# A scheduler flag, and the block inverses of a delta rule: substitution in blocks of 16, the doubling from 16 to 32 on TensorE, and other amounts of filler work between the steps

## The chip, the cores and the metric

The kernel runs on one core of one Trainium2 chip. The metric is device microseconds (us) of one execution. TensorE does the matrix products and the transposes against an identity; VectorE and ScalarE evacuate PSUM, cut weights into two parts and do the elementwise steps; GpSimd (POOL) has a few elementwise operations; SyncE (SP) issues the DMAs. Each engine works its own queue of instructions in order and waits on semaphores of the others.

## The reference

Two layers and a final RMSNorm over 1024 tokens of width 1024, all in float32. The first layer runs dilated window attention beside a gated linear recurrence (HGRN2). The second one, which the change touches, is a gated DeltaNet with 16 value heads over 8 key heads. Cut to what matters here:

```
kb    = kc * beta
lower = where(strict, einsum('id,jd->ij', kb, kc) * decay, 0)   # per head and chunk
a_mat = lower + eye
sol   = triangular_solve(a_mat, [v*beta, kb*exp(gcum)], unit lower)
u, w  = sol[:dv], sol[dv:]
# along the chunks:
v_new = u - w @ state
o     = q_dec @ state + attn_qk @ v_new
state = state * g_last + k_tail.T @ v_new
```

The kernel uses chunks of 128 tokens, forms the inverse of `a_mat` itself (per key head 2 value heads x 8 chunks = 16 matrices of 128x128) and multiplies with it.

## The kernel before, in words

**Arithmetic.** The large projections split each float32 operand into a rounded high part and the rest (`cut`, L112 to L117: ScalarE casts, VectorE subtracts) and take three products (`mm3`, L149 to L153, all of PE L151, L152, L153). One projection of 128 columns over 512 tokens is 24 such matmuls of 128x512.

**Order of the work.** Every stage is a Python generator that yields how much other work it wants behind it (in us, as the author reckons it) and how much it has done itself. `mix(main, fill, scale)` and `blend(side, fill, scale)` interleave such generators, so the program's order is a chain step, then some filler, then the next step. The Tile framework then schedules: it models the engines, picks for each one the earliest instruction in program order that its model says is ready, and so may move instructions forward over ones that it believes still wait. Only in the attention of the first layer is the order of TensorE (for one part VectorE's too) fixed by hand (`manual_schedule`).

**First layer.** Eight HGRN2 heads (`hgrn_chain`): diagonal blocks (`dg`), seven levels of doubling (`lp`, L479 and on; after each one VectorE updates `qt` and `kt`), a transpose (`bk`), chunk states (`kvp`, `S`), outputs (`bops`), a transpose back (`bt`). The filler is the projections of the next head (`hgrn_in`). Then eight pairs of attention heads, an output projection and the norm.

**Second layer.** Per key head `hh` there are three strands, written as

```
fill = proj(hh + 1)                                # projections, convolutions, gates
fill = blend(invert(hh + 1), fill, 0.8)            # the inverses of the next head
mix(recur(hh), fill, 2.8)                          # the recurrence of this head
```

*recur* (L1149): a chain over eight chunks `c`. `ks = kT S` (L1182), VectorE `r` (L1185), `vp = U r` (L1197, U the inverse), VectorE `vt` (L1200) and ScalarE `vn` (L1202), `kv` from `vt` (L1206), VectorE `S` (L1210), then `ks` of the next chunk. Beside it `qk` (L1168) with its evacuation `A` (L1170), `qs` (L1188) with `oq` on ScalarE (L1191), `op` (L1217) with `bv` (L1220).

*invert* (L1044): `kk` (L1063), its evacuation `L` (L1069, 16 operations that need decays `gcl` from ScalarE), the 32x32 diagonal blocks into `Lg`, a transposition into `Lp` (L1078), 31 steps of substitution (two VectorE operations each: a product `tm`, L1084, a subtraction from `Tp`, L1086), transpositions into `Tn` (L1088) and `Un` (L1090). Then two doublings with small matmuls: `qp` (L1107), `Q_`, `up` (L1114, L1115) from 32 to 64, `q2` (L1130) and `u2` (L1138) from 64 to 128. All these results go through the one PSUM buffer with the tag "c". `U` is the tile of `L` itself.

*proj* (L976): per head four convolutions (matmuls `pk`, `pv`, `pq`; VectorE L904 and L908) and, ahead of them, the gates of the head before last (`oz`, `way_out`, L1022): the tile `g` has one buffer, and it comes free when POOL has multiplied it into the head's output, which needs the transposes `ot` (L1012) and, ahead of them, `normed` (L996): a reciprocal root on VectorE and four POOL operations, all behind the last chunk of `recur`.

## Time and profile before

| | |
|---|---|
| three executions | 2271.49, 2265.71, 2271.65 us; median 2271.49 |
| the profiled execution | 2270.35 us |
| its span, first to last instruction | 2268.6 us |
| outside the span | 1.75 us |
| mean granted TensorE clock | 0.992 |
| TensorE, VectorE, ScalarE, POOL busy | 2162.0, 1409.7, 950.0, 239.5 us |
| HGRN2 part of the first layer | about 57 to 540 us |
| attention, output projection, norm | about 540 to 1193 us |
| second layer up to the first `vp` | 1193 to 1317 us |
| its eight recurrences | 1317 to 2105 us |
| the rest | to 2268.6 us |

"Busy" counts a matmul to its modelled end, 0.39 us for one of 128x512, though the next one starts 0.23 us later; so the time in which TensorE gets no new work is larger than the idle time that the page shows. In a waits answer a row says who waited, for whom, the us in total, how often, and the longest. In a timeline row stand the start, the us, the engine, the line, the operation, the tiles, and in brackets the idle time ahead of it and what ended it. `x4` at the end counts merged instructions; a float32 matmul is two of them, a transpose or an fp32r matmul one.

### The profile page before, as it was taken

The page shows a single profiled execution, that of the slowest core. Times are in us where ns is not written, and L with a number is a line of the kernel's source. Part 1 is how long each engine was busy: PE and PEld are TensorE (multiplying, and loading weights), DVE is VectorE, ACT ScalarE, POOL GpSimd, SP SyncE. Part 2 cuts the span into 40 slices and gives each one's busy share as a digit, 9 for nine tenths or more (in the row PEclk, how much of TensorE's full clock was granted, in tenths as well). Part 3 has the DMA queues.
Part 4 walks back from the last instruction along what each step waited for, and adds up shares of the span by engine and source line. Part 5 has one row for each costly group of instructions (what it writes and reads, how often), then busy time and mean ns, then how long its engine had stood idle before and what let it go on. Part 6 is the DMA issues. An engine that isn't in the chain of part 4 may idle for free. (4 is left out here: it accounts for less than half of the span.)

```text
span 2268.6 us, 52553 instructions
## 1 busy us (share of the span) xinstructions
PE 2162.0 (95%) x21781; PEld 1760.6 (78%) x21781; DVE 1409.7 (62%) x3236; ACT 950.0 (42%) x2551; POOL 239.5 (11%) x252
## 2 busy tenths in 40 slices
PE   7999999999999999989999988989898999899998
PEld 6888888898877878767886776767777777678787
DVE  6353535453444344457776986968878787755767
ACT  5233333333232232222237664655555555544223
POOL 0010101010000000000000013121212121210000
PEclk9999999999999999989999999999999999999999
DMA  4111111114342334353233222121212122124233
GB/s 146 38 48 48 43 49 47 48 34 126 91 128 71 109 91 122 97 162 108 93 116 104 61 55 67 51 78 41 77 51 76 49 71 65 58 64 153 85 112 112
DMA packets 100079, 184.15 MB, mean 81 GB/s; under 512 B 12672, under 2 KB 30208, under 8 KB 99840
## 3 DMA queue, kind: packets, MB, share of 16 engines
q1 hardware_dynamic: 99840, 180.79, 25.9%
q8 instruction: 171, 2.80, 0.5%
q14 instruction: 68, 0.56, 0.1%
HBM read 151.25 MB, written 29.49 MB: 80 GB/s over the span
## 5 line engine op out<-in xcount | busy, mean ns | idle before, releaser
L117 DVE TENSOR_TENSOR w_lo<-raww,w_hi 128x512 fp32r<-128x512 f32 x292 | 210.2, 722 | 199.5 <-ACT w_hi L116 196.8
L116 ACT CAST w_hi<-raww 128x512 fp32r<-128x512 f32 x292 | 181.1, 620 | 298.0 <-DMA raww<-in_ewo_dram 51.0
L647 ACT ACTIVATE P<-P,nm 128x256 f32<-128x256 f32 (+7 forms) x128 | 71.4, 559 | 133.9 <-DVE nm L645 133.9
L151 PE MATMUL op<-w_hi,yplo 128*128 128x512 f32 x288 | 113.7, 395 | 3.3 <-DVE hr L296 1.7
L153 PE MATMUL op<-w_hi,yplo 128*128 128x512 f32 x288 | 112.2, 390 | 0.0
L152 PE MATMUL op<-w_lo,yplo 128*128 128x512 f32 x288 | 112.2, 390 | 0.0
L151 PE MATMUL oz<-hn_hi,w_hi 128*128 128x512 f32 x256 | 109.9, 429 | 0.0
L151 PE MATMUL pv<-hn_hi,w_hi 128*128 128x512 f32 x256 | 106.7, 417 | 0.5 <-ACT uv L899 0.5
L296 DVE TENSOR_TENSOR hr<-hr,op 128x512 f32<-128x512 f32 x128 | 85.9, 684 | 34.2 <-PE op L153 33.6
L153 PE MATMUL pv<-hn_hi,w_lo 128*128 128x512 f32 x256 | 104.1, 407 | 0.0
L152 PE MATMUL oz<-hn_lo,w_hi 128*128 128x512 f32 x256 | 103.0, 402 | 0.0
L153 PE MATMUL oz<-hn_hi,w_lo 128*128 128x512 f32 x256 | 102.5, 400 | 0.0
L152 PE MATMUL pv<-hn_lo,w_hi 128*128 128x512 f32 x256 | 102.2, 399 | 0.0
L653 DVE STREAM_TRANSPOSE PB<-P 128x256 f32<-128x256 f32 (+3 forms) x64 | 54.6, 853 | 72.8 <-ACT P L647 72.8
L1156 POOL TENSOR_TENSOR gca<-gca,MA 128x256 f32<-128x256 f32 x64 | 50.6, 791 | 453.8 <-DMA gca<-gcd 252.8
L296 DVE TENSOR_TENSOR hres<-hres,op 128x512 f32<-128x512 f32 x96 | 64.7, 682 | 31.8 <-PE op L153 29.4
L642 DVE CUSTOM_DVE_ANT_0 P<-S,G 128x256 f32<-128x256 f32 (+7 forms) x128 | 58.2, 492 | 36.8 <-PE S L638 35.2
L904 DVE SCALAR_TENSOR_TENSOR vT<-uv,cws,vT 128x512 f32<-128x512 f32 x96 | 74.3, 774 | 4.7 <-ACT vT L902 3.8
L1084 DVE TENSOR_TENSOR tm<-Lp,Tp 128x126 f32<-128x126 f32 (+22 forms) x248 | 74.9, 302 | 3.7
L1158 ACT ACTIVATE gca<-gca,g_ngc 128x128 f32<-128x128 f32 x128 | 45.8, 401 | 69.3 <-POOL gca L1156 69.1
L151 PE MATMUL avp<-w_hi,hn_hi 128*128 128x256 f32 x256 | 74.5, 291 | 0.0
L151 PE MATMUL op<-w_hi,yphi 128*128 128x512 f32 x160 | 65.9, 412 | 8.5 <-ACT yphi L116 4.6
(367 smaller groups left out, 6292.1 us busy)
## 6 DMA issues: line engine op xcount, KB each, us to landing
raww<-in_ew_dram SPq DMA_DIRECT2D x128, 256.0 KB, 3.0
raww<-in_ow_dram SPq DMA_DIRECT2D x100, 256.0 KB, 3.0
V<-vd SPq DMA_DIRECT2D x64, 256.0 KB, 5.3
rawy<-ymix SPq DMA_DIRECT2D x64, 256.0 KB, 2.7
raww<-in_ewo_dram SPq DMA_DIRECT2D x32, 256.0 KB, 3.0
gcl<-gcd SPq DMA_DIRECT2D x64, 128.0 KB, 3.0
gca<-gcd SPq DMA_DIRECT2D x64, 128.0 KB, 3.0
ymix<-oy SPq DMA_DIRECT2D x32, 256.0 KB, 2.0
```

The lines of the kernel that those rows point to most:

```text
L116: act.copy(hi, raw)
L117: dve.tensor_tensor(lo, raw, hi.bitcast(F32), op=ALU.subtract)
L151: pe.matmul(ps, lh, rh, start=start, stop=False)
L152: pe.matmul(ps, lh, rl, start=False, stop=False)
L153: pe.matmul(ps, ll, rh, start=False, stop=stop)
L296: dve.tensor_tensor(dst[:, n], src[:, n], ps, op=ALU.add)
L642: dve.tensor_tensor_reduce(Pm[:, e, w0:], S[e][:, w0:WG], G[:, w0:], 1.0, -3e38, op0=ALU.add, op1=ALU.max, accum_out=mx[:, e:e + 1])
L647: act.activation(Pm[:, e, w0:], Pm[:, e, w0:], AF.Exp, bias=nmx[:, e:e + 1], scale=0.125, accum_out=den[:, i, e:e + 1])
L653: dve.transpose(PB[:, :, i * WG + w0:(i + 1) * WG], Pm[:, :, w0:])
L904: dve.scalar_tensor_tensor(a[0][:, s], ub[:, i + s.start:i + s.stop], cws[:, tile_no, i:i + 1], a[0][:, s], op0=ALU.mult, op1=ALU.add)
L1084: dve.tensor_tensor(tm[:, :31 - k, :n], Lp[:, k, k + 1:, None].to_broadcast([P, 31 - k, n]), Tp[:, k:k + 1, :n].to_broadcast([P, 31 - k, n ...
L1156: pool.tensor_tensor(DA, DA, MA[:, None, :].to_broadcast([P, 2, 128]), op=ALU.add)
```

## The change

Four edits, in `invert`, in the constants and at the program's entry:

1. The substitution works in blocks of 16 instead of 32: 15 steps instead of 31. `Lp` is transposed with 512 elements per partition instead of 1024, and a `copy_predicated` with a new mask `MH` (two columns, loaded once) picks each partition's half. `Tp` starts from a 16x16 identity.
2. The step from 16 to 32 is two more groups of small matmuls: `sp0` (Lg times the lower right inverse), evacuated by ScalarE with the mask into `Q0`, and `sp1` (Tn times Q0), subtracted from `Un` on VectorE, and one more transposition into `Tn`. Each group has 64 matmuls of 32x32 by 16 columns. ScalarE gets two masked copies of `Tp` halves ahead of it. `Un` moves from the tag "Lg" to the tag "Tp".
3. The amounts of filler asked for between the steps of `invert` grow: 15 to 18 behind `kk`, new ones of 1.6, 5.0, 1.6 and 7.0 around `sp0` and `sp1`, 1.5 and 2.0 to 5.0 behind `qp` and `up`, 1.2 to 2.5 behind each half of `q2` and `u2`.
4. `TileContext` gets `schedule_with_timeline_sim=True`: another model of the engines decides what is ready, for the whole program.

```
-                yield (15 if h else 7.0), 0.9
+                yield (18 if h else 7.0), 0.9
...
-            Lp = sp.tile([P, 32, 32], F32, name=f"Lp{hh}", tag="LpQ")
-            dve.transpose(Lp, Lg.rearrange("p u j -> p j u")[:, :, None, :].to_broadcast([P, 32, 2, 16]))
+            Lp = sp.tile([P, 16, 32], F32, name=f"Lp{hh}", tag="LpQ")
+            dve.transpose(Lp, Lg.rearrange("p u (s j) -> p j s u", s=2))
+            dve.copy_predicated(Lp[:, :, 0:16], MH[:, 1:2, None].bitcast(I32).to_broadcast([P, 16, 16]), Lp[:, :, 16:32])
...
-            for k in range(31):
-                n = k // 2 + 1
-                tm = sp.tile([P, 31, 16], F32, name=f"tm{hh}_{k}", tag="tm")
-                dve.tensor_tensor(tm[:, :31 - k, :n], Lp[:, k, k + 1:, None].to_broadcast([P, 31 - k, n]),
...
+            for k in range(15):
+                n = k + 1
+                tm = sp.tile([P, 15, 16], F32, name=f"tm{hh}_{k}", tag="tm")
+                dve.tensor_tensor(tm[:, :15 - k, :n], Lp[:, k, k + 1:16, None].to_broadcast([P, 15 - k, n]),
+                                  Tp[:, k:k + 1, :n].to_broadcast([P, 15 - k, n]), op=ALU.mult)
+                dve.tensor_tensor(Tp[:, k + 1:16, :n], Tp[:, k + 1:16, :n], tm[:, :15 - k, :n], op=ALU.subtract)
+
+            act.mul(Tp[:, 16:32], Tp[:, 0:16], MH[:, 1:2])
+            act.mul(Tp[:, 0:16], Tp[:, 0:16], MH[:, 0:1])
...
-            Un = sp.tile([P, 16, 32], F32, name=f"Un{hh}", tag="Lg")
+            Un = sp.tile([P, 16, 32], F32, name=f"Un{hh}", tag="Tp")
             dve.transpose(Un, Tn)
+
+            blk = [slice(32 * b, 32 * b + 32) for b in range(4)]
+            Q0 = sp.tile([P, 16, 16], F32, name=f"Qs{hh}", tag="LpQ")
+            sp0 = bank("c", [P, 16, 16], f"s0{hh}")
+            for u in range(16):
+                for r in blk:
+                    pe.matmul(sp0[r, u, :], Lg[r, u, :], Un[r, u, 16:32], start=True, stop=True)
+                if u == 7:
+                    yield 1.6, 0.8
+            act.mul(Q0, sp0, MH[:, 0:1])
+            yield 5.0, 0.8
+            sp1 = bank("c", [P, 16, 16], f"s1{hh}")
+            for u in range(16):
+                for r in blk:
+                    pe.matmul(sp1[r, u, :], Tn[r, u, :], Q0[r, u, :], start=True, stop=True)
+                if u == 7:
+                    yield 1.6, 0.8
+            dve.tensor_tensor(Un[:, :, 16:32], Un[:, :, 16:32], sp1, op=ALU.subtract)
+            dve.transpose(Tn, Un)
+            yield 7.0, 0.8
...
-            yield 1.5, 1.3
+            yield 5.0, 1.3
...
-            yield 2.0, 1.8
+            yield 5.0, 1.8
...
-                yield 1.2, 1.7
+                yield 2.5, 0.8
...
-    with tile.TileContext(nc) as tc:
+    with tile.TileContext(nc, schedule_with_timeline_sim=True) as tc:
```

**What the order makes of it.** First, TensorE in the recurrence of head 0, from chunk 3 to chunk 4. `pq` and `oz` are projection matmuls, the other names are those of the recurrence; the number behind an underscore is the chunk. Before:

```order
L1197 MATMUL vp0_3_15878<-r0_3_15853,L0_14534 128x128 x2
L153 MATMUL pq1_1_16098<-hn_hi1_13909,w45_lo3_15245 128x512
L151 MATMUL pq1_1_16098<-hn_hi1_13909,w45_hi3_15244 128x512
L152 MATMUL pq1_1_16098<-hn_lo1_13911,w45_hi3_15244 128x512
L153 MATMUL pq1_1_16098<-hn_hi1_13909,w45_lo3_15245 128x512
L151 MATMUL oz0_0_0_16296<-hn_hi0_13908,w46_hi0_15818 128x512
L1206 MATMUL kv0_3_15907<-vt0_3_15881,kn0_14523 128x256
L152 MATMUL oz0_0_0_16296<-hn_lo0_13910,w46_hi0_15818 128x512
```

and now:

```order
L1224 MATMUL vp0_3_15944<-r0_3_15869,L0_14536 128x128 x2
L1233 MATMUL kv0_3_15991<-vt0_3_15947,kn0_14525 128x256
L1244 MATMUL op0_3_15996<-vn0_3_15949,A0_3_15848 128x128 x2
L1195 MATMUL qk0_4_16004<-q0_15089,kT0_14335 128x128
L1209 MATMUL ks0_4_16041<-S0_3_15993,kT0_14335 128x256
L1215 MATMUL qs0_4_16046<-S0_3_15993,q0_15089 128x256
L1224 MATMUL vp0_4_16099<-r0_4_16043,L0_14536 128x128 x2
```

All projection matmuls have left this stretch; they stand ahead of it, between the steps of `invert(0)`. No projection matmul stands between `vp` of chunk 0 of head 0 and `kv` of chunk 1 of head 1.

Second, TensorE in head 5, at the start of its recurrence. `ot4` are the output transposes of head 4, `oz4` its gates. Before:

```order
L1012 MATMUL ot4_0_1_21299<-ident_69,bv4_19691 128x128 x4
L1182 MATMUL ks5_1_21307<-S5_0_21264,kT5_19401 128x256
L1188 MATMUL qs5_1_21312<-S5_0_21264,q5_21042 128x256
L151 MATMUL oz4_1_0_21317<-hn_hi0_13908,w58_hi2_20863 128x512
L152 MATMUL oz4_1_0_21317<-hn_lo0_13910,w58_hi2_20863 128x512
L153 MATMUL oz4_1_0_21317<-hn_hi0_13908,w58_lo2_20864 128x512
```

(the last three follow each other four times up to `vp5_1`), and now:

```order
L1224 MATMUL vp5_0_21750<-bv5_21433,L5_20316 128x128 x2
L1233 MATMUL kv5_0_21798<-vt5_0_21753,kn5_19865 128x256
L1244 MATMUL op5_0_21802<-vn5_0_21755,A5_0_21724 128x128 x2
L1195 MATMUL qk5_1_21810<-q5_21578,kT5_19599 128x128
L1209 MATMUL ks5_1_21843<-S5_0_21800,kT5_19599 128x256
L1015 MATMUL ot4_0_0_21742<-ident_69,bv4_20126 128x128 x2
L1215 MATMUL qs5_1_21848<-S5_0_21800,q5_21578 128x256
L1015 MATMUL ot4_0_0_21742<-ident_69,bv4_20126 128x128 x2
L1015 MATMUL ot4_0_1_21835<-ident_69,bv4_20126 128x128 x2
L1224 MATMUL vp5_1_21866<-r5_1_21845,L5_20316 128x128 x2
```

The gates `oz4` up to `oz4_1_0` stand ahead of `vp5_0` now; the next projection matmul comes behind `qs5_2`. From there on 18 to 27 projection matmuls stand in most links, where 6 to 12 stood before.

Third, VectorE in head 5, around `r` of chunk 2. `A5_2` and `bv5` are evacuations of the recurrence, `tm6`, `Tp6` the substitution of head 6. Before:

```order
L1220 TENSOR_TENSOR bv5_20909<-op5_1_21366,oq5_1_21314 128x256
L1084 TENSOR_TENSOR tm6_3_21423<-Lp6_21410,Tp6_21412 128x28x2
L1086 TENSOR_TENSOR Tp6_21412<-Tp6_21412,tm6_3_21423 128x28x2
L1084 TENSOR_TENSOR tm6_4_21426<-Lp6_21410,Tp6_21412 128x27x3
L1086 TENSOR_TENSOR Tp6_21412<-Tp6_21412,tm6_4_21426 128x27x3
L1084 TENSOR_TENSOR tm6_5_21429<-Lp6_21410,Tp6_21412 128x26x3
L1086 TENSOR_TENSOR Tp6_21412<-Tp6_21412,tm6_5_21429 128x26x3
L1084 TENSOR_TENSOR tm6_6_21432<-Lp6_21410,Tp6_21412 128x25x4
L1086 TENSOR_TENSOR Tp6_21412<-Tp6_21412,tm6_6_21432 128x25x4
L1084 TENSOR_TENSOR tm6_7_21435<-Lp6_21410,Tp6_21412 128x24x4
L1185 SCALAR_TENSOR_TENSOR r5_2_21398<-ks5_2_21396,sc5_19547,bv5_20909 128x128 x2
```

and now:

```order
L1237 SCALAR_TENSOR_TENSOR S5_1_21899<-S5_0_21800,g_egl_14223,kv5_1_21897 128x128 x2
L1081 STREAM_TRANSPOSE Lp6_21977<-Lg6_21624 128x512
L1082 COPY_PREDICATED Lp6_21977<-MH_14226,Lp6_21977 128x16x16
L1088 TENSOR_TENSOR tm6_0_21982<-Lp6_21977,Tp6_21980 128x15
L1090 TENSOR_TENSOR Tp6_21980<-Tp6_21980,tm6_0_21982 128x15
L1247 TENSOR_TENSOR bv5_21433<-op5_1_21902,oq5_1_21850 128x256
L1088 TENSOR_TENSOR tm6_1_21985<-Lp6_21977,Tp6_21980 128x14x2
L1197 TENSOR_TENSOR A5_2_21912<-qk5_2_21910,gca5_2_21805 128x256
L1090 TENSOR_TENSOR Tp6_21980<-Tp6_21980,tm6_1_21985 128x14x2
L1212 SCALAR_TENSOR_TENSOR r5_2_21934<-ks5_2_21932,sc5_19861,bv5_21433 128x128 x2
```

The substitution starts ahead of `r5_2` in both; now it is over before `S` of chunk 2, and before it reached into the later chunks.

In the whole program TensorE passes from one shape of array tile to another 564 times now, 436 times before: 374 against 334 in the first layer, 190 against 102 in the second. Without edit 4 the second layer has 144. The order of the attention stage is the same but for its first pair.

More of the change, by code (lines that the diff above doesn't have):

```diff
@@ L39 @@
 C_T0 = C_ID32 + 32
-C_PM = C_T0 + 512
+C_MH = C_T0 + 256
+C_PM = C_MH + 2
 C_ALL = C_PM + 128
@@ L72, in const_table @@
     c[:, C_ID32:C_ID32 + 32] = j[:, None] == np.arange(32)[None, :]
-    i, j = np.arange(32)[:, None], np.arange(16)[None, :]
-    for par in range(2):
-        c[(p // 16) % 2 == par, C_T0:C_T0 + 512] = (i == 2 * j + par).reshape(-1)
+    c[:, C_T0:C_T0 + 256] = np.eye(16).reshape(-1)
+    for half in range(2):
+        c[(p // 16) % 2 == half, C_MH + half] = 1.0
     c[p, C_PM + q] = 0.5
@@ L821, in odd_layer @@
         nc.sync.dma_start(MA, cst[:, C_MA:C_MA + 128])
+        MH = sp.tile([P, 2], F32, name="MH")
+        nc.sync.dma_start(MH, cst[:, C_MH:C_MH + 2])
         cws = sp.tile([P, 32, 4], F32, name="cws")
```

8 lines of the change are left out of this document (3 added, 5 removed).

## The prediction

> **What bounds the kernel now.** I read the page first, then PE's waits, then the windows by stage. The page gives the engines and, in 40 slices, their shares:
>
> ```profile
> PE 2162.0 (95%) x21781; PEld 1760.6 (78%) x21781; DVE 1409.7 (62%) x3236; ACT 950.0 (42%) x2551; POOL 239.5 (11%) x252
> PE   7999999999999999989999988989898999899998
> DVE  6353535453444344457776986968878787755767
> PEclk9999999999999999989999999999999999999999
> ```
>
> TensorE is the bound almost everywhere. In the second layer (from slice 22 on) PE alternates between eights and nines, and there VectorE rises to eights and nines too. So the first question is whether TensorE gets more or less work, the second what it loses in waits there. Windows say how evenly: columns are the stretch, its length, busy us (with instructions) of PE, weight loads, DVE, ACT, POOL, then the granted clock, the DMA share and GB/s. They are the HGRN2 part, the front of the second layer, and heads 2, 3 and 4:
>
> ```profile
> 57.00:540.00 483.00, 481.27 (x5994) 411.82 (x5994) 219.29 (x402) 172.26 (x443) 48.15 (x42) 1.00 0.15 50
> 1193.00:1317.00 124.00, 116.56 (x776) 89.72 (x776) 103.29 (x260) 80.19 (x207) 7.39 (x10) 1.00 0.25 73
> 1596.00:1704.00 108.00, 99.96 (x700) 80.87 (x699) 85.45 (x224) 60.89 (x184) 21.57 (x24) 1.00 0.21 62
> 1704.00:1811.00 107.00, 99.66 (x700) 80.78 (x699) 85.09 (x224) 60.72 (x183) 21.25 (x24) 1.00 0.21 63
> 1811.00:1919.00 108.00, 99.93 (x700) 80.76 (x698) 87.30 (x226) 61.78 (x185) 21.11 (x24) 1.00 0.23 66
> ```
>
> The HGRN2 part leaves 1.7 us of 483; nothing can be won there. A steady head leaves 7 to 8 us of 108. No engine is full in it: VectorE has 85 of 107.5. It is lost in the chain, as PE's waits between 1264 and 2000 show (us in total, times, longest):
>
> ```profile
> PE op L1217 <- ACT vn L1202: 10.1, 13, 1.6
> PE ks L1182 <- DVE S L1210: 9.7, 7, 1.8
> PE vp L1197 <- ACT oq L1191: 7.2, 10, 1.6
> PE vp L1197 <- DVE r L1185: 3.9, 4, 1.0
> ```
>
> One link in the timeline of head 4 shows why (start, length, engine):
>
> ```profile
> 1833.18 0.67 PE L1182 MATMUL ks<-S,kT 128*128 128x256 f32 x2
> 1833.62 0.38 DVE L1084 TENSOR_TENSOR tm<-Lp,Tp 128x56 f32<-128x56 f32 x1
> ...
> 1835.99 0.26 DVE L1084 TENSOR_TENSOR tm<-Lp,Tp 128x96 f32<-128x96 f32 x1
> 1836.16 0.60 DVE L1185 SCALAR_TENSOR_TENSOR r<-ks,sc,bv 128x128 f32<-128x128 f32 x2
> 1836.65 0.68 PE L1197 MATMUL vp<-r,L 128*128 128x128 f32 x4 [0.98 <-DVE r L1185]
> ```
>
> `ks` ends at 1833.85, `r` starts only at 1836.16: VectorE works off substitution steps that stand ahead of it in the queue, and PE runs dry for 0.98 us.
>
> **The sum, against the profiled run** (2270.35 us, 1.14 under the median of the three, 2271.49). 0.3% is about what a measurement of this kernel can tell from no change.
>
> *New matmuls.* 128 per head, two instructions each, 8 heads: 2048. No row has 32x32 by 16 columns; the nearest ones are
>
> ```profile
> L479 PE MATMUL lp<-bqt,bkt 128*32 128x16 f32 x2560 | 29.4, 185 | 1.7 <-DVE bkt L505 1.6
> L1114 PE MATMUL up<-Q,Tn 32*32 32x32 f32 x512 | 9.6, 192 | 4.6 <-DVE Q L1109 4.6
> L1107 PE MATMUL qp<-Un,L 32*32 32x32 f32 x512 | 10.3, 197 | 3.4 <-DVE Un L1090 2.3 <-DVE rt L199 0.6 <-DVE rt L198 0.5
> ```
>
> The busy time, merged over tiles that run at once, is 29.4/2560 = 11.5 ns an instruction for 16 columns, 18.8 for `up` and 20.1 for `qp` with 32 columns. I take 11.5, the row with the same columns: **+23.6**; with 20.1 it is +41, which is the upper end, and half the lower price, +12, is the lower one.
>
> The Trainium skill, "TensorE: Matmul & The Clock Gate", section "Wait — 56ns, not 53.3ns?", has start to start never below about 25 ns, however few columns. By that these would be 51 us, an estimate, and the sum 28 higher; the rows above disagree, as 11.5 to 20.1 ns an instruction shows.
>
> *Changes of the tile shape.* 128 more. After small tiles the next full matmul starts later than in a row of full ones:
>
> ```profile
> 1302.54 1.20 PE L1107 MATMUL qp<-Un,L 32*32 32x32 f32 x64 [0.49 <-DVE rt L198]
> 1303.67 0.50 PE L153 MATMUL pv<-hn_hi,w_lo 128*128 128x512 f32 x1
> 1304.01 0.39 PE L151 MATMUL pv<-hn_hi,w_hi 128*128 128x512 f32 x1
> 1304.24 0.40 PE L152 MATMUL pv<-hn_lo,w_hi 128*128 128x512 f32 x1
> ```
>
> 0.34 against 0.23 us, so 0.1 each: **+12.8** (0 to 25).
>
> *VectorE.* Removed is half of these two groups and some:
>
> ```profile
> L1084 DVE TENSOR_TENSOR tm<-Lp,Tp 128x126 f32<-128x126 f32 (+22 forms) x248 | 74.9, 302 | 3.7
> L1086 DVE TENSOR_TENSOR Tp<-Tp,tm 128x126 f32<-128x126 f32 (+22 forms) x248 | 69.4, 280 | 3.5
> L1078 DVE STREAM_TRANSPOSE Lp<-Lg 128x1024 f32<-128x1024 f32 x8 | 16.2, 2027 | 9.1 <-ACT Lg L1076 9.1
> L1088 DVE STREAM_TRANSPOSE Tn<-Tp 128x512 f32<-128x512 f32 x8 | 9.2, 1148 | 0.1
> L1090 DVE STREAM_TRANSPOSE Un<-Tn 128x512 f32<-128x512 f32 x8 | 5.6, 700 | 0.0
> ```
>
> Per head 144.3/8 = 18.0 for 62 operations; 30 operations of at most 64 elements at about 0.21 are 6.3. `Lp` falls from 2.03 to about 1.0; the new select, subtraction and third transposition are about 0.45, 0.4 and 0.7. So VectorE goes from 22 to about 10.5 us, 11.6 less per head, 85 to 74 of 107.5. None of it is on the path by itself; it shortens the links in which `r`, `vt` or `S` stand behind it.
>
> *Stalls.* I counted each head's PE instructions at their undisturbed start to start (0.23 for 512 columns as above; 288 of them are 66 us, the rest 28): 93.7 us in a steady head, of the 107.6 from one first `vp` to the next, (1919.34 − 1488.98)/4:
>
> ```profile
> 1488.98 0.38 PE L1197 MATMUL vp<-bv,L 128*128 128x128 f32 x2
> ...
> 1919.34 0.61 PE L1197 MATMUL vp<-bv,L 128*128 128x128 f32 x4
> ```
>
> The gap, 13.9, is larger than the 7 to 8 of the windows because busy runs to the modelled end (0.39) of a matmul. Then I took each of the 21 links of a head (`vt` to `S`, `S` to `r`, `r` to `vt`, and the one to the next head) as the longest of three: PE's work between them, VectorE's, and the bare chain. Before, these sum to 106.5, 1% under the trace, a fair model. In the new order they sum to 104.4, with 97.3 of PE work; times 1.015 that is 106.0, a stall of 8.7 instead of 13.9. So four steady heads give −21. It is not more because filler now sits in lumps: links with 18 to 27 projection matmuls (4 to 6 us) stand beside empty ones, where the bare chain, about 4.5 us a chunk, decides. Heads 6 and 7 give −7 by the same count, heads 0 and 1 only −5, since head 0 has no filler (its chunks have 1.7 us of PE work against a chain of 3.5 to 5.5) though 13 us less work. Ahead of head 0, where that work went (+28 us of PE between the first projection and `vp`), the waits fall from 19.6 to 11.6, −8. Together **−41**, between −73 and −11 (the rivals).
>
> *First layer.* In HGRN2, 26 projection matmuls now stand between the levels of a head, 12 before, and nearly none at its end. The only wait in the levels is small:
>
> ```profile
> PE lp L479 <- DVE bkt L505: 1.6, 3, 0.9
> ```
>
> The ends of heads wait for ScalarE and VectorE evacuations instead; I take **+3** (0 to 16, 2 us for each of eight heads).
>
> *Clock.* Behind a stretch with idle time the granted clock halved:
>
> ```profile
> 1366.00:1379.00 13.00, 9.15 (x46) 6.77 (x44) 12.68 (x44) 4.97 (x17) 5.03 (x6) 1.00 0.13 41
> 1379.00:1389.30 10.30, 8.18 (x83) 6.45 (x83) 7.48 (x14) 3.04 (x5) 7.32 (x10) 0.50 0.24 78
> ```
>
> The starved head 0 makes this likelier: **+4** (0 to 22).
>
> *At nothing.* ScalarE's three short operations, about 0.4 each, lie in the 47 us that it idles in a head. `sp0` waits for `Un`, `sp1` for ScalarE's `Q0`; behind the waiting matmul stand the recurrence's own `ks` and `vp`, and the 5 and 7 us of filler asked for ahead of it cover this; without cover about 1 us each, 16 in all. The load of `Tp` waits on SP's queue for the last reader of the former `Un`, with weight loads behind it; that reader is done most of a head, 107 us, earlier. The load of `MH` is hidden by the start of the layer.
>
> 2270.35 + 23.6 + 12.8 − 41 + 3 + 4 = 2272.75, **2273**: no change that can be told. Added PE work of 36 us is paid back by shorter waits.
>
> **Rivals.** *A, faster.* The link model has no carry-over: PE that finishes a lump early leaves nothing to the next link. If the order's lumps let VectorE and ScalarE run ahead (VectorE has 11.6 us more slack), the steady heads lose only about 1 us each: 4 x 7.7 = 31, and the time is 2273 − 32 = 2241. For it: three of the four wait rows above name an evacuation standing behind other work, not a bare chain. Against it: the link model met the trace of before within 1% without any carry-over.
>
> *B, slower.* The start of each head is starved. The filler that stood there (`oz` of the head before) stands ahead of `vp` now, and `normed` (13 short VectorE operations, 2.2 us at
>
> ```profile
> L199 DVE TENSOR_TENSOR ort<-ort,ors 128x16 f32<-128x16 f32 x3 | 0.5, 173 | 0.1
> ```
>
> each) and the packed substitution, about 10 us, stand in VectorE's queue among `vt`, `S` and `r` of chunks 0 to 2. PE has 6 to 7 us of rows from `vp` of chunk 0 to `ks` of chunk 2. At 5 us lost in each of six heads it is +30: 2303. It decides when this stretch takes more than about 12 us. For it: VectorE runs in order and the link above shows 2.3 us of delay by five such operations. Against it: the new scheduler has a timeline of the engines, and placed `r` of chunk 2 behind only two steps of substitution.
>
> *C, slower by the clock.* The half clock covers head 0's starved 44 us, where 16 us of PE work take twice as long and half of that hides in waits, +8, and five head starts, each like the quoted stretch (8.18 us of work at half clock, 4.1 at the full one; two thirds of the difference reach the chain, 2.8): +14. Less the 4 counted, 2291. For it: the quoted row. Against it: the dip came once in 2268 us at this depth.
>
> The Trainium skill, "TensorE: Matmul & The Clock Gate", section "What's actually happening", has windows of about 3.4 us and half rate behind an idle one; by that rule head 0 would run at half. The trace agrees with the 0.50 of the row above.
>
> That the change does nothing is excluded: the order differs in the whole program.
>
> **Chances.** Forecast 0.40 (own range 2255 to 2290, its terms' bounds partly offsetting; 0.11 of it faster, 0.17 the same, 0.12 slower), A 0.30, B 0.18, C 0.12. The stall term holds most of the uncertainty and the model behind it was tested on one order only, so A has nearly as much as the forecast. Faster 0.11 + 0.30 = 0.41, same 0.17, slower 0.12 + 0.18 + 0.12 = 0.42. The range reaches to both A and B with some 6 us beyond each, 2235 to 2310.
>
> **What would show it.** `sp0` and `sp1` groups at about 12 ns an instruction (23 to 25 us in all; at 20 the first term fails). Steady heads of 106 us from `vp` to `vp`: 98 is rival A, 111 with waits at `ks` and `vp` of chunks 0 to 2 is B. PEclk below 8 in head 0 is C. HGRN2 over 3 us longer, with waits at the ends of heads, breaks the fourth term. The whole is wrong if the time leaves 2255 to 2290.

## The result and the profile after

The changed kernel takes 2389.22 us (median of four, 2379.22 to 2391.54), the kernel before beside it 2270.68. The ratio is 1.0518, 95% interval 1.0483 to 1.0553: 5% slower, 118.5 us. The forecast was 2273, the range ended at 2310.

The first page of the profile after, the same lines as shown of before:

```profile
span 2389.8 us, 56378 instructions
PE 2253.5 (94%) x23829; PEld 1833.4 (77%) x23829; DVE 1358.0 (57%) x3004; ACT 955.4 (40%) x2573; POOL 231.3 (10%) x252
PE   7999999999999999899999978989898989999998
DVE  5344444443444444466767755767666766755667
PEclk9999999999999999899999968989999999999999
```

TensorE is still busy for 94%, but 91.5 us longer, although only 22 us of small matmuls are new. PEclk shows a part of the reason: the slice of head 0 is granted 0.6, where before no slice fell below 0.8. A matmul at half clock is busy for longer: the four `vp` instructions of a chunk take 1.22 us at 1429.59 us, where the granted clock is 0.50, and 0.61 us at 1681.60 us, where it is full. The split below puts 42 us on the clock. TensorE's idle time grew from 106.6 to 136.3 us only. VectorE is busy for 51.7 us less.

The windows of the HGRN2 part, the front of the second layer, and heads 0, 3 and 4 (columns as in the prediction):

```profile
57.00:546.00 489.00, 488.45 (x6025) 420.61 (x6031) 218.83 (x412) 169.27 (x443) 42.69 (x40) 1.00 0.14 47
1212.00:1376.00 164.00, 154.15 (x1168) 119.67 (x1167) 113.09 (x258) 93.87 (x232) 7.29 (x10) 0.97 0.22 60
1376.00:1448.00 72.00, 53.20 (x621) 40.04 (x619) 37.27 (x113) 30.51 (x105) 9.22 (x14) 0.61 0.12 31
1681.60:1800.00 118.40, 108.87 (x949) 88.11 (x947) 77.89 (x190) 59.35 (x178) 19.59 (x23) 0.94 0.17 53
1800.00:1917.80 117.80, 109.00 (x963) 88.36 (x964) 79.43 (x199) 64.31 (x194) 20.99 (x23) 0.96 0.21 58
```

A steady head takes 118 us instead of 107.5. VectorE falls there from 85 to 78 or 79 us, and it buys nothing in sight. By stages, from the starts of the first gate matmul and of each head's first `vp` (flag alone is edit 4 on the kernel before, no flag is the changed kernel without edit 4, no groups leaves the new small matmuls out as well; runs e1, e2 and e5 below):

| us | before | changed | flag alone | no flag | no groups |
|---|---|---|---|---|---|
| up to the second layer | 1193.1 | 1212.4 | 1209.4 | 1193.2 | 1194.0 |
| its front, up to `vp` | 124.5 | 164.0 | 164.5 | 111.1 | 106.9 |
| heads 0 and 1 | 171.4 | 188.7 | 190.2 | 194.6 | 178.8 |
| heads 2 to 5, each | 107.6 | 117.5 | 113.3 | 110.2 | 106.4 |
| heads 6 and 7, to the last `vp` | 185.8 | 191.0 | 184.6 | 182.8 | 180.4 |

I also split each kernel's TensorE time in three: work is each instruction at the lower quartile of the start to start that its pair of shapes has in the kernel before (11 ns or less for the new shape); what it takes beyond that while the granted clock is 0.50, up to double, is clock; the rest is stall, ordinary small gaps included. So only differences count:

| us | before | changed | flag alone | no flag | no groups |
|---|---|---|---|---|---|
| work | 1937 | 1960 | 1938 | 1950 | 1935 |
| clock | 11 | 53 | 58 | 20 | 9 |
| stall | 304 | 359 | 352 | 300 | 288 |

Against before, the changed kernel has +23 of work, +42 of clock and +55 of stall. The same split by stages (its sums agree with the table within 4 us), changed less before:

| us | work | clock | stall |
|---|---|---|---|
| up to the second layer | 0 | +6 | +13 |
| its front, up to `vp` | +29 | +4 | +6 |
| heads 0 and 1 | −13 | +13 | +18 |
| heads 2 to 5, each | +3 | +4 | +2.5 |
| heads 6 and 7 | −2 | +3 | +4 |
| the rest | −4 | 0 | +3 |

Inside heads 2 to 5 chunks 0 and 1 lose about 5 us of stall and 2.5 of clock in each head; the later chunks give about 2.5 of the stall back.

The waits of TensorE in the changed kernel from 1325 to 2119 (who waited, for whom, us, times, longest):

```profile
PE vp L1224 <- ACT oq L1218: 16.9, 15, 2.8
PE kv L1233 <- DVE vt L1227: 14.6, 13, 5.1
PE op L1244 <- ACT vn L1229: 10.1, 6, 2.4
PE ot L1015 <- ACT oy L1016: 8.8, 6, 3.1
PE ot L1015 <- POOL bv L1008: 6.7, 2, 4.1
```

The waits at `ks` for `S` and at `kk` for `L` (9.7 and 5.7 us before, from 1264 to 2000) have left the top of the list; those at `vp` for ScalarE's `oq` have more than doubled (7.2 before), and `kv` and `ot` are new among the long ones. The start of head 3 in the timeline shows what kind of wait they are:

```profile
1681.60 0.61 PE L1224 MATMUL vp<-bv,L 128*128 128x128 f32 x4
...
1683.21 0.69 ACT L1057 ACTIVATE gcl<-gcl,g_ngc 128x128 f32<-128x128 f32 x2 [1.98 <-DMA gcl<-gcd]
...
1684.57 0.72 POOL L1183 TENSOR_TENSOR gca<-gca,MA 128x256 f32<-128x256 f32 x1 [18.80 <-DMA gca<-gcd]
...
1685.19 1.12 DVE L1072 SCALAR_TENSOR_TENSOR L<-kk,sc,gcl 128x128 f32<-128x128 f32 x4 [1.65 <-ACT gcl L1058]
...
1686.23 0.41 DVE L1227 TENSOR_TENSOR vt<-vp,g_etl 128x256 f32<-128x256 f32 x1
1686.35 0.69 PE L1015 MATMUL ot<-ident,bv 128*128 128x128 f32 x2 [4.14 <-POOL bv L1008]
...
1686.83 0.67 PE L1233 MATMUL kv<-vt,kn 128*128 128x256 f32 x1
```

`vp` ends at 1682.2, and `vt` could follow at once. But VectorE has `normed` and then `L` of the next head ahead of it; `L` waits for ScalarE, ScalarE for a transfer. On TensorE `ot` stands ahead of `kv` and waits for GpSimd, which waited for another transfer. Four queues, each in order, each with an early instruction at its head that is not ready.

### The profile page after: what moved, and what is told of

Its sections match the earlier page's. It is cut to its first block, busy times and chain, and to the rows that moved or that the text cites. A ratio compares the mean times of both kernels' runs of the same rounds, so it can differ in the third digit from the quotient of the medians.

```text
span 2389.8 us, 56378 instructions
## 1 busy us (share of the span) xinstructions
PE 2253.5 (94%) x23829; PEld 1833.4 (77%) x23829; DVE 1358.0 (57%) x3004; ACT 955.4 (40%) x2573; POOL 231.3 (10%) x252
## 5 line engine op out<-in xcount | busy, mean ns | idle before, releaser
L152 PE MATMUL oz<-hn_hi,w_hi 128*128 128x512 f32 x256 | 105.0, 410 | 0.7 <-DVE g L995 0.6
L152 PE MATMUL bip<-w_hi,hn_hi 128*128 128x256 f32 x256 | 73.3, 286 | 0.0
```

What stands on the lines that cost most here:

```text
L152: pe.matmul(ps, lh, rh, start=start, stop=False)
```

## The experiments

**The two parts apart.** Four runs: edit 4 alone (e1), edits 1 to 3 alone (e2), and the changed kernel with the old amounts of filler (e3 without the flag, e4 with it).

```
-    with tile.TileContext(nc) as tc:                                   # e1, on before
+    with tile.TileContext(nc, schedule_with_timeline_sim=True) as tc:
```

> The kernel before with edit 4 (the scheduler's flag) alone. Theory O (the order: the flag takes the filler out of head 0 and out of the start of every head, so that TensorE stalls there and its granted clock halves behind each stall): most of the 119 us remain, since only the new small matmuls (22 us of TensorE) are gone, so 2340 to 2380 us, granted clock at or below 0.97, head 0 about 70 us long with hardly any projection matmul. Theory N (the new steps cost: two more groups of small matmuls with their waits in the recurrence, the order matters little): 2255 to 2290 us, clock about 0.99.

> The changed kernel without edit 4: substitution in blocks of 16, the new doubling and the larger amounts of filler, in the order of the old scheduler, which keeps 6 to 12 projection matmuls in each link of the recurrence. Theory O: near the kernel before: +22 us of small matmuls and +4 of tile shapes against shorter links in the steady heads (the longest-of-three sum gives 105.6 against 106.5 per head), so 2270 to 2300 us with clock about 0.99. Theory N: 2340 to 2390 us.

> The changed kernel without edits 3 and 4: the old amounts of filler, and 1.5 us each at the two new steps. What the larger amounts bring in the old order. Theory O: the steps of the inverse follow each other sooner and end a chunk earlier, the longest-of-three sum is 102.9 per steady head, so within 15 us of the run with the larger amounts, either way: 2255 to 2295 us. Theory N: the waits of the new steps have less cover, 10 to 40 us above the run with the larger amounts.

> The changed kernel without edit 3 (old amounts of filler), with the flag. Theory O: the starved head 0 and the starved head starts remain, so 2370 to 2400 us, clock at or below 0.97. Theory N: as the changed kernel plus what the missing cover costs, 2395 to 2430 us.

Measured: e1 2368.59 us, ratio 1.0409 (1.0392 to 1.0425), granted clock 0.960; e2 2289.91, 1.0062 (1.0046 to 1.0077), 0.987; e3 2303.11, 1.0118 (1.0093 to 1.0142); e4 2379.54, 1.0463 (1.0440 to 1.0485). The kernel before beside them took 2276.53.

The diff of e3 and e4 against e2 and the changed kernel:

```
-                yield (18 if h else 7.0), 0.9
+                yield (15 if h else 7.0), 0.9
...
-                if u == 7:                             # in both groups
-                    yield 1.6, 0.8
...
-            yield 5.0, 0.8                             # behind Q0; behind sp1: 7.0
+            yield 1.5, 0.8
...                                                     # qp, up, q2, u2 as before
```

So the flag costs 92 us by itself and 99 on top of the other edits; edits 1 to 3 cost 13. The kernel before took between 2270.7 and 2276.5 us from one set of runs to the next, so a difference between runs of different sets is known to some 6 us only: with each run set against the kernel before beside it, the 99 are 105. Theory N has fallen, since e1 alone holds most of the loss. The larger amounts of filler are worth 13 us without the flag (e3 less e2, at the lower end of what theory N named for this run) and cost 10 to 16 with it. Head 0 of the flag alone, and its head 3:

```profile
1373.90:1458.30 84.40, 60.50 (x395) 43.86 (x396) 50.21 (x154) 35.58 (x113) 17.78 (x22) 0.62 0.14 38
1677.40:1789.60 112.20, 103.64 (x699) 85.09 (x699) 83.61 (x224) 59.93 (x184) 19.92 (x23) 0.95 0.20 59
```

The clock of 0.62 is there without a single one of the new small matmuls. Head 0 takes 84 us there, not the 70 that theory O named.

**What the small matmuls cost, and what VectorE's saving brings.** e5 takes the two groups out, e9 issues each twice; both without the flag.

```
-            for u in range(16):                       # e5; sp1 goes too, Q0 is subtracted in its place
-                for r in blk:
-                    pe.matmul(sp0[r, u, :], Lg[r, u, :], Un[r, u, 16:32], start=True, stop=True)
-            act.mul(Q0, sp0, MH[:, 0:1])
+            act.mul(Q0, Un[:, :, 16:32], MH[:, 0:1])
```

```
-                for r in blk:                         # e9, the same for sp1
+                for r in blk * 2:
```

> The changed kernel without the flag and without its two groups of 32x32 matmuls (it leaves out the product that joins the 16x16 blocks: Q0 is a masked copy of Un, and it is subtracted in place of the product). All of VectorE's saving stays, the order stays. If the 14 us by which the version without the flag is slower than before are the price of the groups on TensorE (theory P: VectorE's saving of 11.6 us a head is off the path, so it buys at most 1 to 2 us a head): 22 to 30 us below that version, 2260 to 2270 us, 5 to 15 below the kernel before. If the price is in the waits and lumps of the new order (rival W): 2280 to 2292 us.

> The version without the flag, with every 32x32 matmul of the two new groups issued twice in place (2048 more TensorE instructions, no more changes of the tile shape, the order of all else the same). If they cost what the nearest row of the trace of before says, 11.5 ns an instruction: +24 us, 2314. If a rule of 25 ns an instruction holds: +51 us, 2341. If they fit into time in which TensorE waits anyway: 0 to +10 us.

Measured: e5 2248.82 us, 0.9888 (0.9875 to 0.9902), 25 us below the kernel before; e9 2341.78, 1.0298 (1.0284 to 1.0312), 52 above e2. The groups therefore cost 41 us where they are, with their shape changes, waits and clock (20 us of half clock loss with them, 9 without), and VectorE's saving, with the larger amounts of filler and the order that comes with both, is worth 25. Both are larger than either theory had it; their difference, 16, is what e2 is slower by (13 us in its own comparison).

The second 2048 instructions cost 25 ns each. Their rows, in e2 and then in e9:

```profile
L1112 PE MATMUL s<-Qs,Tn 32*32 32x16 f32 x1024 | 11.7, 180 | 2.9 <-issue 2.9
L1104 PE MATMUL s<-Un,Lg 32*32 32x16 f32 x1024 | 10.1, 180 | 5.1 <-DVE Un L1097 4.3 <-DVE cq L940 0.7
```

```profile
L1112 PE MATMUL s<-Qs,Tn 32*32 32x16 f32 x2048 | 25.3, 191 | 6.4 <-issue 6.4
L1104 PE MATMUL s<-Un,Lg 32*32 32x16 f32 x2048 | 21.2, 183 | 22.8 <-issue 19.2 <-DVE Un L1097 2.7 <-DVE cq L940 0.7
```

Busy doubles, 22 to 46.5, and the wait "issue", in which TensorE waits for nothing that the profile shows, grows from 2.9 to 25.6 us. Of the 25 ns some 12 are busy time and 11 are this wait. One burst of 256 in the timeline of e9:

```profile
1666.59 1.81 PE L1104 MATMUL s<-Un,Lg 32*32 32x16 f32 x186
1670.83 1.15 PE L1104 MATMUL s<-Un,Lg 32*32 32x16 f32 x70 [2.44 <-issue]
```

186 instructions start within 1.6 us, 8.8 ns apart, then nothing for 2.4 us, then the rest.

**Is the half clock a cause or a sign?** e6 keeps TensorE's array busy in head 0. The code is shortened; the tiles `ks` and `vp` are twice as wide for it:

```
+                    for _ in range(2 if hh == 0 else 0):          # behind qs
+                        pe.matmul(ks[:, 2:4], kT[:, s], St, start=True, stop=True)
...
+                for _ in range(2 if hh == 0 else 0):              # behind vp
+                    pe.matmul(vp[:, 2:4, :], U[:, 2 * c, :], r_, start=True, stop=True)
```

> The changed kernel with four more full-width matmuls (128x256, results unused) in each chunk of the recurrence of head 0, two behind ks and qs, two behind vp, where TensorE would wait for VectorE: about 27 us more TensorE work in a stretch that takes 72 us at a granted clock of 0.61. Theory C (the half clock itself lengthens head 0, by 13 us, and it is granted back as soon as the array is kept busy): the clock of this stretch rises above 0.85 and the stretch gets no longer than 72 us, perhaps 62 to 70, in spite of 27 us more work. Rival (the chain of waits alone sets the length, the clock is a by-product): 75 to 95 us, whatever the clock.

Measured: 2379.12 us, 1.0462 (1.0448 to 1.0477). Head 0 of the changed kernel, then that of e6:

```profile
1376.40:1448.20 71.80, 52.80 (x619) 39.73 (x617) 37.47 (x114) 30.52 (x106) 9.22 (x14) 0.61 0.12 31
```

```profile
1371.60:1440.00 68.40, 52.31 (x696) 39.39 (x694) 36.92 (x111) 30.86 (x105) 9.26 (x14) 0.93 0.13 32
```

The clock rises from 0.61 to 0.93, and head 0 is 3.4 us shorter with more work. The expectation reckoned that work too high: it is 60 instructions at about 0.24 us (four of them from 1405.94 to 1406.91 in its timeline), 14 us, not 27. So the half clock is a cause, as theory C had it. Of the 13 us that it holds in head 0 by the split above at least 3.4 reach the end of the head; how much more the added work hid isn't shown. The order of the other heads also moved a little, so the rest of its gain over the changed kernel isn't read as clock.

**Does the wait at the head's start cost what it shows?** e7 moves `way_out` behind the first pair of convolutions.

```
-            if j > 1:
-                yield from way_out(j - 2)
             w = unit()
...
+            if j > 1:
+                yield from way_out(j - 2)
             w = unit()
```

> The changed kernel with the gates and output transposes of the former head placed behind the first pair of convolutions of each projection instead of ahead of it (the weights follow in that order). Theory B (at a head's start the transposes ot stand in TensorE's queue behind vp of chunk 0, wait 4 us for GpSimd, and projection work is out of reach): filler stands at the head starts, the waits for GpSimd at ot go, and the half clock behind them: steady heads 110 to 113 us instead of 117, 2350 to 2372 us in all. Rival (vt of chunk 0 waits behind VectorE's queue anyway, and the loss only moves): within 10 us of the changed kernel, 2380 to 2400 us.

Measured: 2392.09 us, 1.0512 (1.0495 to 1.0528), no change. The wait for GpSimd from 1565 to 1918, which is heads 2 to 4 of the changed kernel, first there:

```profile
PE ot L1015 <- POOL bv L1008: 4.1, 1, 4.1
```

and then e7's waits of TensorE in the same window, which name GpSimd nowhere:

```profile
PE vp L1224 <- ACT oq L1218: 8.8, 6, 3.2
PE vp L1224 <- DVE A L1197: 6.6, 3, 3.1
PE tk L920 <- DVE kT L911: 3.8, 3, 1.7
```

The wait for GpSimd is gone and `vp` waits instead. It was a single one in three heads, and one of two from 1325 to 2119, so it couldn't hold what theory B put on it. In e7 31 to 71 projection matmuls do stand behind `vp` of chunk 0 in heads 2 to 5, where the changed kernel has none, but only 0 to 12 behind that of chunk 7 (0 to 43 there), and these heads take 118.9 us each. Theory B falls, and the rival's forecast that the loss only moves is met.

**Starving by hand.** Without the flag: e10 draws head 0's filler ahead of it, e11 asks for no filler in chunks 0 and 1 of heads 1 to 6.

```
-        drain(blend(invert(0), fill, 0.8))                             # e10
+        drain(blend(invert(0), seq(fill, proj(1)), 0.8))
...                                                     # head 0 has only invert(1) as filler, scale 0.6
```

```
-            mix(recur(hh), fill, 2.8)                                  # e11
+            mix(recur(hh), fill, *((4.2, 7) if 0 < hh < 7 else (2.8, 0)))   # 7 steps with none
```

> The version without the flag, with the projections of the next head drawn ahead of the recurrence of head 0 by hand, as the flag's order does, so that chunks 3 to 7 of head 0 have no filler. Theory O (the flag costs because the filler is spent early and is missed later): the granted clock halves in these chunks and the stretch from the first projection to the first vp of head 2, 305.7 us without the flag and 352.7 in the changed kernel, grows by 20 to 45 us; 2310 to 2335 us in all. Rival (the starved head costs little, since the work done earlier is saved later): 2285 to 2300 us.

> The version without the flag, in heads 1 to 6 with no filler asked for in the first seven steps of the recurrence (chunks 0 and 1) and 1.5 times as much in the others, as the flag's order has it. The sum of work is the same. Theory O: each of these heads loses 4 to 8 us in the first two chunks, in waits and half clock, 24 to 45 us in all: 2314 to 2335 us. Rival (filler at one place is as good as at another): within 10 us of the version without the flag, 2280 to 2300 us.

Measured: e10 2301.02 us, 1.0124 (1.0109 to 1.0139); e11 2300.67, 1.0121 (1.0104 to 1.0139): 11 us each above e2, 15 when each is set against the kernel before beside it. Both lie below theory O's ranges and 1 us above the rivals'.

e10 has the mechanism in part: chunks 4 to 7 of head 0 are left without projection matmuls, the granted clock from chunk 3 on is 0.80 (0.51 in the changed kernel, 0.93 in e2), and the stretch up to the first `vp` of head 2 grows from 305.7 to 320.6 us. e11 doesn't have it. The scheduler moved filler back, so that 14 and 11 projection matmuls stand in chunks 0 and 1 of heads 2 to 6, where the changed kernel has none in four of five chunks 0; the granted clock is 1.00 in these two chunks (0.69 to 0.87 in chunk 0 of the changed kernel), and by the split they lose nothing against e2. What e11 loses stands in chunk 3, where the first small matmul waits in a lump of filler for the substitution. In its heads 2 to 4:

```profile
PE s L1104 <- DVE Un L1097: 12.7, 3, 4.3
```

So e11 says nothing on the price of the flag's own starved head starts, and theory O is neither shown nor refuted by these two runs.

**TensorE's order or the others'?** e13 keeps the flag and fixes TensorE's order of the second layer as the program writes it, e14 does the same without the flag, e15 on the kernel before.

```
+        with tc.manual_schedule(engines={mybir.EngineType.PE}):
             fill = blend(gates(), start())
...
```

> The changed kernel with the flag, but TensorE's instructions of the second layer (from the gates to the end of the eight heads) kept in the order in which the program writes them, 6 to 12 projection matmuls in nearly every link; the other engines and the first layer as the flag orders them. The hand-made starvations cost 11 us each of the 99 that the flag costs, so where the rest lies is open. Theory O (TensorE's order): the 80 us that the second layer loses with the flag go almost wholly, 2295 to 2320 us, the rest being the 19 us of the first layer. Rival Q (the flag's order of VectorE, ScalarE, GpSimd and the DMA queue: operations that wait stand ahead of vt, r and oq): 2350 to 2390 us.

> The version without the flag with TensorE's instructions of the second layer in the order in which the program writes them. The measure for the run above: the two differ in the first layer (19 us) and in the flag's order of the other engines alone. Theory O: within 12 us of the version without the flag (2290), and 15 to 30 us below the run above. Rival Q: the same here, but 60 to 100 us below the run above.

> The kernel before with TensorE's instructions of the second layer in the order in which the program writes them: no projection matmul is moved ahead by the scheduler. If the scheduler's small moves are worth nothing: 2268 to 2280 us. If they fill waits that the written order leaves: 2285 to 2310 us; this also says what the written order alone costs in the two runs above.

Measured: e13 2447.94 us, 1.0770 (1.0756 to 1.0785); e14 2381.22, 1.0475 (1.0460 to 1.0489); e15 2434.59, 1.0716 (1.0698 to 1.0733). The times that were expected of all three missed: the written order is bad by itself, 91 us without the flag and 161 in the kernel before. Only rival Q's difference came out, 60 to 100 us between e14 and e13: it is 67. The waits that do it, first in e15, then in e14:

```profile
PE qp L1107 <- DVE Un L1090: 166.5, 8, 26.4
```

```profile
PE s L1104 <- DVE Un L1097: 74.5, 8, 13.0
```

The first small matmul stands in the queue until the substitution is through, up to 26 us a head. In this order edits 1 to 3 win 53 us (e15 less e14), since the substitution is shorter; in the kernel before, the scheduler's moves hide most of it already.

But e13 and e14 have the same order on TensorE in the second layer, and the flag costs 67 us between them: 17 ahead of that layer, the rest in it. In e13, then in e14:

```profile
PE vp L1224 <- ACT oq L1218: 30.6, 17, 5.8
PE op L1244 <- ACT vn L1229: 20.4, 9, 2.8
```

```profile
PE vp L1224 <- ACT oq L1218: 13.6, 19, 1.7
PE op L1244 <- ACT vn L1229: 2.6, 3, 1.3
```

With one order on TensorE, ScalarE's `oq` and `vn` come later under the flag, and these two rows alone differ by 35 us. By the split the loss in heads 1 to 6 lies in chunk 0: 8 to 10 us of stall in e13, 3 to 4 in e14, with the same projection matmuls in it; later chunks give some of it back. So in the written order some 50 us come from the order of the other engines, the DMA queue among them, as rival Q says. The changed kernel loses at the same place (6 to 7 us of stall in chunk 0 of heads 2 to 5, 3 to 4 before), but that it is by the same waits and to the same amount is argued, not shown. The converse, those engines as written and TensorE free, was not tried.

**Taking the late transfer away.** ScalarE waits ahead of `gcl` for its transfer; e16 to e18 give it four buffers and issue it two chunks earlier.

```
-        g = sp.tile([P, 2, 128], F32, name=f"gc{w}{hh}_{c}", tag=f"gc{w}", bufs=2)
+        g = sp.tile([P, 2, 128], F32, name=f"gc{w}{hh}_{c}", tag=f"gc{w}", bufs=4 if w == "l" else 2)
...
+            early_l = [decays(hh, c, "l") for c in range(2)]
...
-                gcB = decays(hh, c, "l")
+                gcB = early_l.pop(0)
+                if c + 2 < NT:
+                    early_l.append(decays(hh, c + 2, "l"))
```

> The changed kernel with the decay tiles gcl of the inverse in four buffers instead of two and their transfers issued two chunks earlier (the tile oy pays for it, one buffer instead of two). ScalarE idles 65 us ahead of its operations on gcl until that transfer lands, 46 us in the version without the flag, and oq and vn stand behind them. Theory Q (under the flag a good part of the loss is ScalarE and VectorE waiting in order for this transfer ahead of oq, vn and vt): that idle time falls below 20 us, and the time falls by 20 to 45 us, 2345 to 2370 us. Rival (other operations wait in its place, the loss is in TensorE's filler): 2380 to 2395 us.

> The version without the flag with the same edit. TensorE waits 12.8 us there at kk for L, which waits for gcl. If that goes and nothing takes its place: 2272 to 2284 us; if other waits do: 2284 to 2294 us.

> The kernel before with the same edit, as a try for a version that beats both: TensorE waits 5.7 us at kk for L between 1264 and 2000 and ScalarE idles 37.5 us for the transfer. If these waits end there: 2260 to 2267 us; if the filler covers them already: 2267 to 2277 us.

Measured: e16 2379.20 us, 1.0463 (1.0449 to 1.0478); e17 2303.34, 1.0132 (1.0118 to 1.0147); e18 2284.40, 1.0055 (1.0041 to 1.0069). ScalarE's wait in the changed kernel, then in e16:

```profile
ACT gcl L1057 <- DMA gcl<-gcd: 64.6, 44, 5.7
```

```profile
ACT gcl L1061 <- DMA gcl<-gcd: 47.3, 29, 4.3
```

The wait fell by a quarter only, not below 20 us, so the edit didn't take the late transfer away. The time fell by 10 us, to 1 us below the rival's range and far from theory Q's. Without the flag the edit costs 11 us (e18) to 13 (e17), more than was expected, and the wait hardly falls, from 37.5 to 37.6 and from 45.9 to 41.6 us. That the edit gains with the flag and costs without it agrees with theory Q, the size doesn't settle it.

**Tries for a faster version.** e8 puts the larger amounts of filler on the kernel before, e12 leaves the new groups unsplit in the version without the flag, with 8 us of filler asked for ahead of `sp1`.

```
-            yield 1.5, 1.3                             # e8, behind qp; the others of edit 3 too
+            yield 5.0, 1.3
```

```
-                if u == 7:                             # e12, in both groups
-                    yield 1.6, 0.8
...
-            yield 5.0, 0.8
+            yield 8.0, 1.6
...
-            yield 7.0, 0.8
+            yield 7.0, 1.6
```

> The kernel before with the larger amounts of filler of edit 3 alone, at the steps that it has. TensorE's waits for the evacuations L, Q and L of the inverse took 15 us from 1264 to 2000 in the kernel before. If the amounts cover them: 2255 to 2268 us. If the filler is only taken from other links, where it is missed: 2268 to 2290 us.

> The version without the flag, with the two new groups not split in halves by filler (32 fewer changes of the tile shape) and 8 in place of 5 us of filler asked for ahead of sp1. A try for a version that beats the kernel before. If the shape changes and the wait for Q0 hold most of what the groups cost beyond their own time: 2270 to 2282 us. If not: 2285 to 2295 us.

Measured: e8 2280.76 us, 1.0033 (1.0020 to 1.0045); e12 2291.12, 1.0083 (1.0067 to 1.0099). Neither helps. No version with the whole computation beat the kernel before.

## Why the prediction was wrong, step by step

**The step that failed is the stall term**, "Together **−41**". By the split the stall grew by 55 us, and it is the flag's (+48 alone, −4 without it). Some 13 of the 55 lie ahead of the second layer, which the prediction priced apart; the rest, about +41, stands against its −41: +6 in the front (−8 forecast), +18 in heads 0 and 1 (−5), +10 in heads 2 to 5 (−21), +4 in heads 6 and 7 (−7), +3 behind them. The counts of TensorE's work came out in the same stages: +29 in the front (28 forecast), −13 in heads 0 and 1 (13), +3 in a steady head (3.6). So the step from work to time failed. The link model took the longest of TensorE's work, VectorE's work and the bare chain. An engine that stands still at the head of its queue, because the next instruction in order waits for something else, is in none of the three. The order on record showed the signs, `ot4` ahead of `vp5_1` and the projection matmuls gone from the first chunks, but not who waits for whom. That the model met the trace of before within 1% was no test: its purpose is to tell two orders apart, and it had seen one. Which of the waits hold how much of the +41 stays open.

**The clock term**, +4, measured +42 by the split. Rival C named the mechanism and the places, with a price of 22 before the 4 are taken off, 8 in head 0 and 14 at five head starts. Measured are +10 in head 0 (13 against 3) and +15 in chunks 0 and 1 of heads 1 to 6; the other 17 or so stand ahead of head 0 and in later chunks. e6 shows that the clock in head 0 is a cause of at least 3.4 us. The Trainium skill, "TensorE: Matmul & The Clock Gate", section "What's actually happening", has windows of about 3.4 us after which the rate changes. The trace agrees: between 1200 and 2200 us the half-clock stretches of the changed kernel last 3.4, 6.8 or 10.2 us, and one that begins in head 0 lasts 51.2, all multiples of 3.41.

**New matmuls and shape changes**, 23.6 + 12.8 = 36.4: the groups measured 41 where they stand (e2 less e5, so without the flag). Near in sum, and the 22.4 us busy in the changed kernel fit the row of `lp`. The Trainium skill, "TensorE: Matmul & The Clock Gate", section "Wait — 56ns, not 53.3ns?", has no start to start below about 25 ns, which the prediction set aside because of its rows. Single starts here are 8.5 ns apart, against it. 2048 more of them did cost 52 us, 25 ns each, but as 12 ns of busy time and 11 of pauses in long bursts, so as far as these runs show the agreement is luck.

**VectorE**: the two groups of the substitution in the changed kernel are

```profile
L1088 DVE TENSOR_TENSOR tm<-Lp,Tp 128x15 f32<-128x15 f32 (+7 forms) x120 | 32.0, 266 | 2.9
L1090 DVE TENSOR_TENSOR Tp<-Tp,tm 128x15 f32<-128x15 f32 (+7 forms) x120 | 30.3, 252 | 2.8
```

62.3/240 = 0.26 us an operation, not the 0.21 of the sum, so 7.8 us a head instead of 6.3, and the whole saving was put too high: VectorE is busy for 78 or 79 us of a steady head, not 74. "None of it is on the path by itself" held for the steady heads (106.4 without the groups against 107.6). The 25 us of e5 are 20 in the profiled executions: about 10 up to the end of head 1, 5 in heads 2 to 5, 5 in heads 6 and 7 by the table.

**First layer**, +3 in HGRN2: HGRN2 itself took 1.7 more (467.1 to 468.8 from the first `dg` to the first score), but all that lies ahead of the second layer 19.3. The norm ahead of it, the first pair of attention heads (58.0 to 65.7) and the rest of the attention (595.1 to 600.8) had no price at all. By the split the 19.3 are 13 of stall and 6 of clock; no run asks which waits they are.

**Rivals.** B had the place right, and by the split the price as well: chunks 0 and 1 of heads 2 to 5 lose about 5 us of stall each. Its sign doesn't tell the two kernels apart: from `vp` of chunk 0 to `ks` of chunk 2 the changed kernel takes 14.7 to 19.8 us in heads 2 to 5, over the 12 that it named, but the kernel before takes 20 to 23, full of filler. C's sign came, PEclk of 6 in head 0. B and C were set against each other as alternatives; they come together: head 0, where TensorE waits most, is also where the clock falls most, to 0.61. With both, 2273 + 30 + 18 = 2321, the sum still lay outside the range, and 11 us above its upper end. It keeps the forecast's saving of 41 in all other places, which didn't come, and 3 us for the first layer, which lost 19. What was missing was a case in which the new order is worse everywhere. (In rival A, 4 x 7.7 is 31, and 32 were taken off.)

What stays open: of the flag's 99 us about 19 lie ahead of the second layer, and in the written order some 50 come with the order of the engines beside TensorE (e13 less e14, without the 17 ahead of the layer). How much of the rest in the changed kernel is that order and how much is the missing filler isn't settled.

## What to carry to other kernels

Another scheduling model touches the order of the whole program, whatever else a change holds; put it on alone first (it was 92 of 118 us here). An order is judged by what stands at the head of each in-order queue and what that waits for, transfers included; sums of busy time per link don't show it. And in a kernel whose TensorE is 95% busy, taking work from VectorE for 256 more TensorE instructions a head was a loss by itself: 25 us won, 41 paid.

## What the runs showed of the hardware that was not expected

A burst of small matmuls runs at 8.5 ns an instruction at full clock, but each of the eleven bursts of 256 in e9 stops between the 109th and the 255th instruction, nine of them once for 2.2 to 2.8 us from one start to the next, with "issue" as the only reason. Of e2's eleven bursts of 128 three stop, for 0.6 to 1.5 us, and of the changed kernel's none. Why isn't known from these runs. And a busy TensorE is no sign of a full clock: in head 0 of the changed kernel

```profile
1426.00:1436.00 10.00, 9.70 (x259) 8.10 (x260) 5.79 (x12) 2.74 (x10) 4.36 (x7) 0.50 0.10 24
```

it is 97% busy, about half of it with 32x32 tiles and the rest with recurrence matmuls, and the granted clock stays at 0.50.
